# One table function for gelu, a fused bias and minimum in the scores, and probabilities scaled on ScalarE, in a two-layer encoder

## The chip, the cores and the metric

The kernel runs on one core of a Trainium2 chip. A core has five engines with queues of their own: TensorE (PE) for matmuls, VectorE (DVE) and ScalarE (ACT) for elementwise work, GpSimd (POOL), and SyncE (SP), which here issues DMAs. Each queue is worked off in order; semaphores tie the queues together. The metric is the device time of one execution in microseconds, the median over several runs.

## The reference

Two layers, each with two sub-layers, on one sequence of 256 tokens with 1024 channels in float32, then a last norm. Sub-layer 1 mixes tokens: one projection gives pooled groups, queries, keys and values of twelve heads in three dilation groups, and two gates. Sub-layer 2 is a gated MLP of width 2816 with a depthwise convolution of three tokens. What the change touches:

```python
# attention, for each head: logits with a bias, masked, a softmax
logits = jnp.einsum('bqhd,bqkhd->bhqk', qb, kb) * scale
logits = logits + bias[None, :, None, :]
logits = jnp.where(valid[None, None], logits, NEG_INF)
lse = jax.nn.logsumexp(logits, axis=-1)
p = jnp.exp(logits - lse[..., None])
o = jnp.einsum('bhqk,bqkhd->bqhd', p, vb)
...
wts = jax.nn.softmax(jnp.stack(lses, axis=0), axis=0)
...
merged = jax.nn.sigmoid(g_pool) * (pool_out @ w_a) + jax.nn.sigmoid(g_attn) * (attn_out @ w_b)
...
# the MLP: gelu is jax's default, the tanh form
a, gval = jnp.split(xn @ w_up, 2, axis=-1)
a = lax.conv_general_dilated(a, conv_w[:, None, :], ...) + conv_b
return (jax.nn.gelu(a) * gval) @ w_down
```

The three groups' outputs are combined by their softmax denominators, which is the same as one softmax over the concatenated logits of the three groups.

## The kernel before

Every matmul runs on float32 data in a faster format (float32r) and is split into a high and a low part, with three products (high by high, high by low, low by high). So each weight piece that comes from memory is split first: ScalarE casts the high part (`wh`, line 201), VectorE subtracts to get the low part (`wl`, line 203). The class `Weights` keeps that stream: loads from memory (three buffers `raw`, issued by SyncE), splits of pieces in the order of their use, up to three pieces ahead of the matmul that asks for one (`LOOK`), in at most five buffers (`BUFS`). A piece is 128 rows by 1024 columns' worth; `proj` (line 543) and `by_tokens`/`v_sum` (line 667) use it up, in 16 and 12 matmuls. The MLP's way down goes through `residual_mm` and `row_mm` (lines 585 to 587).

The program is written in the order in which the work is meant to happen, tile by tile; the framework orders the instructions of each engine, derives the semaphores, and `tc.issue_after` adds wishes by hand ("not before this one").

Attention in each layer: the projections of the six pairs of heads (`PAIRS`) run while a dictionary `steps` spreads the work of the four head slots (each with one head of each of the three groups) over twenty places. `scores(hh)` makes, for each of the two halves of tokens, a 128 by 512 tile of logits in PSUM (lines 1029 and 1034), adds the bias (`bias_of`, a strided view of a table; line 1040), takes the negated maximum of each row (line 1045), then the exponential with its sum (line 1048), the reciprocal of the sum (line 1050), and scales the probabilities by it and by one half (line 1051). That half comes from the gates: a sigmoid is made as half of (1 + tanh). `start_turn` transposes the probabilities in blocks on VectorE and sends them through memory with DMAs (`cross`, lines 711 to 718); `turn` splits the dense group's part into high and low (`pth` line 1072, `ptl` line 1073); `weigh` multiplies them with the values (lines 1082 and 1086) and splits the sum (`at2`, lines 1091 and 1092), which `by_tokens` uses later. Line 1131 and its neighbours evacuate the projections of queries and keys. `gate` (line 1160) makes the tanh of the gates.

The MLP works on 22 chunks of 128 channels. `up(f)` gets the chunk's activation from PSUM (`add_up`, lines 579 and 580; the first four come by another path, line 1266), makes the convolution (lines 1274, 1275 and 1278), then gelu out of a square (line 1288), a step on VectorE (1289), a tanh (1292) and another step (1293), multiplies by the gate's value and by one half (line 1297, or 1303 for the last two chunks) and splits the product (lines 1308 and 1309). The way down follows six chunks behind (`LAG`).

Line 756 is the first use of ScalarE at the start, line 771 the sum of squares of the input, line 918 the values' scaling by the first norm, line 372 a row of matmuls ahead of the real ones, lines 445 to 524 the residual sums and the last norm.

Of the kernel before, what the change touches and what calls it, by code (L numbers as in the profile page):

```python
# [10 lines left out]
F32 = mybir.dt.float32  # L11
F32R = mybir.dt.float32r
AF = mybir.ActivationFunctionType
ALU = mybir.AluOpType
AX = mybir.AxisListType

P = 128
# [224 lines left out]
def encoder(ctx, tc, x, w_in, w_pool, pool_scale, w_a, w_b, w_o, norm1, norm2, w_up, conv_w,  # L242
            conv_b, w_down, rel_bias, norm_f, onehot, edges, out):
    nc = tc.nc
# [3 lines left out]
    sm = ctx.enter_context(tc.tile_pool(name="small", bufs=2))  # L248
# [24 lines left out]
    for l in range(DEPTH):  # L273
        for g in range(NG):
            c0 = C_V + g * 512
            slots = (("m2", 0, 2), ("m2", 1, 2), ("ybig",), ("at2",)) if g == 0 else ()
            for j in range(2):
                tag = "k1" if l == 0 and g == 1 and j == 0 else None
# [25 lines left out]
        for j in range(2):  # L304
            tag = None if j else "k1"
# [4 lines left out]
        for f in range(4, NF, 2):  # L310
            if f in HALF_GROUPS:
                n, j = HALF_GROUPS[f]
                W.use(rows(w_up[l], j * 512, 4, DFF + n * 512, 512))
            a = cols(w_up[l], f * P)
            if f >= 4 * NQ:
                g = cols(w_up[l], DFF + f * P)
                a = [a[0], g[0], a[1], g[1]]
# [107 lines left out]
    def bias_of(t, hh):  # L425

        b = bt[:, hh]
        (pstep, pn), _ = b.ap
        blocks, first = (-2 * P, 4 * P - 1) if t == 0 else (-3 * P, 5 * P - 1)
        return bass.AP(b.tensor, b.offset + first, [[pstep, pn], [blocks, 2], [-1, 256]])  # L430
# [142 lines left out]
    def in_order(a):  # L573

        return a.rearrange("p (m t) -> p t m", t=2)
# [327 lines left out]
    for l in range(DEPTH):  # L903
# [25 lines left out]
        else:  # L929
            for g in range(NG):  # L930
                held = begun[0] if g == 0 else [W.get() for _ in range(4)]
                for t in range(2):
                    if g + t == 0:
                        ps = begun[1]
                    else:
                        ps = v_tile()
# [6 lines left out]
        if l == 0:  # L943
            load_params()
            with tc.issue_after(W.behind[1].ins):
                bias = build_bias()
# [6 lines left out]
        for gi in range(3, -1, -1):  # L953
# [12 lines left out]
            while sh < w:  # L966
# [3 lines left out]
                    out=nxt[:, :, 0:n], in0=cur[:, :, 0:n], in1=cur[:, :, sh : sh + n]  # L970
# [7 lines left out]
            if hw > 1:  # L978
# [5 lines left out]
                out=pd, in0=cur[:, :, o : o + S], scalar=1.0 / w, in1=u[:, :, PAD : PAD + S],  # L984
                op0=ALU.mult, op1=ALU.subtract,
# [39 lines left out]
        def scores(hh):  # L1025
            for t in range(2):
                ps = acc.tile([P, 512], F32, tag="acc", name="s_ps")
                for m, (a, b) in enumerate(((qh, kh), (qh, kl), (ql, kh))):
                    nc.tensor.matmul(  # L1029
                        ps[:, 0:256], a[:, hh, t, :], b[:, hh].rearrange("p t m -> p (t m)"),  # L1030
                        start=(m == 0), stop=(m == 2),
                    )
                for g in (1, 2):
                    nc.tensor.matmul(  # L1034
                        ps[:, 128 + g * 128 : 256 + g * 128], q[:, (g - 1) * HPG + hh, t, :],
                        kk[:, (g - 1) * HPG + hh, t, :],
                        start=True, stop=True,
                    )
                s = sm.tile([P, 512], F32, tag="s", name="s")
                nc.vector.tensor_add(  # L1040
                    out=s.rearrange("p (a b) -> p a b", a=2), in0=ps.rearrange("p (a b) -> p a b", a=2),
                    in1=bias_of(t, hh),
                )
                nm = sm.tile([P, 1], F32, tag="nm", name="nm")
                nc.vector.tensor_reduce(out=nm, in_=s, axis=AX.X, op=ALU.max, negate=True)
                z = sm.tile([P, 1], F32, tag="z", name="z")
                p = sm.tile([P, 512], F32, tag="p", bufs=3, name="p")
                nc.scalar.activation(p, s, AF.Exp, bias=nm[:, 0:1], accum_out=z)
                rz = sm.tile([P, 1], F32, tag="rz", name="rz")
                nc.vector.reciprocal(rz, z)  # L1050
                nc.vector.tensor_scalar(
                    out=p, in0=p, scalar1=rz[:, 0:1], scalar2=0.5, op0=ALU.mult, op1=ALU.mult
                )
                probs[hh, t] = p


# [19 lines left out]
        def weigh(hh):  # L1076
            pth, ptl, pt = ptiles[hh]
            ps = acc.tile([P, 2, P], F32, tag="acc", name="o_ps")
            for kc in range(2):
                c = slice(hh * P, (hh + 1) * P)  # L1080
                for m, (a, b) in enumerate(((vh, pth), (vh, ptl), (vl, pth))):
                    nc.tensor.matmul(ps, a[:, kc, c], b[:, kc], start=(kc + m == 0), stop=False)  # L1082
            for g in (1, 2):
                hd = (g - 1) * HPG + hh
                for t in range(2):
                    nc.tensor.matmul(  # L1086
                        ps[:, t, :], v[:, t, hd * P : (hd + 1) * P], pt[:, 4 * t : 4 * t + 4, 1 + g, :],
                        start=False, stop=(g == 2 and t == 1),
                    )
            oh, ol = at2[:, hh, 0], at2[:, hh, 1]  # L1090
            nc.scalar.copy(out=oh, in_=ps)
            nc.vector.tensor_sub(out=ol, in0=ps, in1=oh.bitcast(F32))


        steps = {
# [19 lines left out]
        for m, c in enumerate(PAIRS):  # L1115
# [7 lines left out]
            for n in range(4):  # L1123
# [4 lines left out]
                scale = HD**-0.5 if n < 2 else 1.0  # L1128
                if hd < HPG:
# [3 lines left out]
                        out=lo[:, hd], in0=src, scalar=scale, in1=hi[:, hd].bitcast(F32),  # L1133
                        op0=ALU.mult, op1=ALU.subtract,
                    )
                    nc.vector.scalar_tensor_tensor(
                        out=lo[:, hd], in0=rest, scalar=scale, in1=lo[:, hd].bitcast(F32),
                        op0=ALU.mult, op1=ALU.add,
                    )
                else:  # L1140
# [3 lines left out]
                        out=o, in0=src, scalar=scale, in1=o, op0=ALU.mult, op1=ALU.add  # L1144
# [6 lines left out]
        for cc in HALVES:  # L1151
            ps = by_tokens(po2, 4, then=step)
# [10 lines left out]
        for cc in HALVES:  # L1163
# [4 lines left out]
            for t in range(2):  # L1168
                nc.vector.scalar_tensor_tensor(
                    out=pa[:, t, cc], in0=th[:, t], scalar=1.0, in1=pa[:, t, cc],  # L1170
                    op0=ALU.add, op1=ALU.mult,
# [5 lines left out]
        for n, cc in enumerate(HALVES):  # L1177
            th = gate()
            ps = by_tokens(at2, 2, 2)
            ks = slice(4 * n, 4 * n + 4)  # L1180
            y = big.tile([P, 2, 4, 4, 32], F32, tag=("q0", "k0")[n], name="turned")
            z = big.tile([P, 2, 4, 4, 32], F32, tag=("q1", "v0")[n], name="merged")
# [53 lines left out]
        z_of = [zg[:, 0], zg[:, 1], zga[:, 0]]  # L1236
# [6 lines left out]
        def of_chunk(z, i):  # L1243
            return z[:, :, i].rearrange("p (t a) j -> p t a j", t=2)
# [17 lines left out]
        def up(f):  # L1262
            w0, w1, w2, b = (prm[:, l, j * NF + f : j * NF + f + 1] for j in range(4))
            a = sm.tile([P, S], F32, tag="u", name="a")
            if f < 4:
                nc.scalar.copy(
                    out=a.rearrange("p (a j t) -> p t a j", t=2, j=32), in_=of_chunk(za, f)
                )
            else:
                sums = proj(x2, 2)  # L1270
                with W.after_splits():
                    add_up(in_order(a), [halves(b) for b in sums])
            y = sm.tile([P, S], F32, tag="s", name="y")
            nc.scalar.activation(y, a, AF.Identity, bias=b, scale=w1)
            nc.vector.scalar_tensor_tensor(
                out=y[:, 1:], in0=a[:, : S - 1], scalar=w0, in1=y[:, 1:], op0=ALU.mult, op1=ALU.add
            )
            nc.vector.scalar_tensor_tensor(
                out=y[:, : S - 1], in0=a[:, 1:], scalar=w2, in1=y[:, : S - 1],
                op0=ALU.mult, op1=ALU.add,  # L1280
            )
            g = sm.tile([P, 2, P], F32, tag="p", bufs=3, name="g")
            if f >= 4 * NQ:
                add_up(g, [halves(a) for a in proj(x2, 2)])

            c = float(np.sqrt(2.0 / np.pi))
            y2 = sm.tile([P, S], F32, tag="us", name="y2")
            nc.scalar.activation(y2, y, AF.Square, scale=float(np.sqrt(0.044715)))
            nc.vector.scalar_tensor_tensor(
                out=y2, in0=y2, scalar=1.0, in1=y, op0=ALU.add, op1=ALU.mult  # L1290
            )
            nc.scalar.activation(y2, y2, AF.Tanh, scale=c)
            nc.vector.scalar_tensor_tensor(
                out=y2, in0=y2, scalar=1.0, in1=y, op0=ALU.add, op1=ALU.mult
            )
            if f < 4 * NQ:
                nc.vector.scalar_tensor_tensor(  # L1297
                    out=g.rearrange("p t (a j) -> p t a j", j=32),
                    in0=y2.rearrange("p (a j t) -> p t a j", t=2, j=32), scalar=0.5,
                    in1=of_chunk(z_of[f // 4 % 3], f % 4), op0=ALU.mult, op1=ALU.mult,  # L1300
                )
            else:
                nc.vector.scalar_tensor_tensor(
                    out=g, in0=in_order(y2), scalar=0.5, in1=g, op0=ALU.mult, op1=ALU.mult
                )
            n = f % NH
            ah, al = (x[n >= HPG][:, n - HPG * (n >= HPG)] for x in (acth, actl))
            nc.scalar.copy(out=ah, in_=g)  # L1308
            nc.vector.tensor_sub(out=al, in0=g, in1=ah.bitcast(F32))
            acts[f] = (ah, al)  # L1310
# [64 lines left out]
```

## Time and profile before

| What | Value |
|---|---|
| time before, median of 3 runs | 859.94 us |
| the three runs | 859.94, 860.45, 859.87 us |
| span of the profiled execution, first to last instruction | 858.0 us |
| granted TensorE clock, mean over the span | 0.998 |
| DMA | 186.81 MB, 218 GB/s on average |
| one instruction of the table loads of ScalarE (ACT_TABLE_LOAD) | 1 in the whole run |

The profile is a record of one execution. The page gives the busy time of each engine, the chain of work that ended last, and groups of instructions by line. "PE" is TensorE's matmuls, "PEld" its weight loads, which overlap them. In a row of a group, `x44 | 17.8, 420 | 1.6 <-ACT y L1292 0.8` says: 44 instructions, 17.8 us busy, 420 ns each on average; before them the engine sat idle for 1.6 us, 0.8 us of it until ScalarE's line 1292 was done. A row of the chain in order of time gives the start in us, the length in us, and what ran. A row of the timeline gives start, length, engine, line, operation, tiles and shapes, how many are merged, and in brackets the idle time before. A row of the waits names who waited for whom: total us, times, longest.

### The profile page before, as it was taken

The numbers are of one execution on the slowest core, as the hardware profiler recorded it, in microseconds if no ns is written. First come the engines' busy times: TensorE is split into PE (matmuls) and PEld (weight loads), VectorE is DVE, ScalarE is ACT, GpSimd is POOL, SyncE is SP. The second block draws the span as 40 slices with busy tenths as digits, with TensorE's granted clock in tenths as the row PEclk, the third lists the DMA queues.
The fourth block names the chain that finished last, engine by engine and source line by source line (L and its number), as shares of the span: only waits on it lengthen the run. The fifth ranks groups of instructions, "written<-read, shape, count | busy, mean of one in ns | idle before, by whom it ended". The sixth has DMA issues, their size and how long they took to land.

```text
span 858.0 us, 11823 instructions
## 1 busy us (share of the span) xinstructions
PE 851.6 (99%) x4343; PEld 727.9 (85%) x4343; DVE 661.2 (77%) x1050; ACT 493.8 (58%) x795; POOL 32.0 (4%) x98
## 2 busy tenths in 40 slices
PE   9999999999999999999999999999999999999997
PEld 8888888888888888888888889988888888888886
DVE  7998796667767788888855987874776777988894
ACT  7756654455445476666645665543654555775672
POOL 1710000000010000000000000000000000000001
PEclk9999999999999999999999999999999999999999
DMA  9686547766747876666736555658667478676641
GB/s 331 217 248 206 196 163 231 240 228 229 250 182 246 270 249 231 231 235 206 245 99 209 184 199 192 198 175 268 226 243 275 154 249 259 246 256 208 239 147 49
DMA packets 136387, 186.81 MB, mean 218 GB/s; under 512 B 5561, under 2 KB 88193, under 8 KB 136329
## 3 DMA queue, kind: packets, MB, share of 16 engines
q1 hardware_dynamic: 136168, 185.79, 63.8%
q8 instruction: 34, 0.56, 0.3%
q10 hardware_dynamic: 160, 0.27, 0.1%
q14 instruction: 25, 0.20, 0.1%
HBM read 172.39 MB, written 13.65 MB: 217 GB/s over the span
## 4 chain that ended last, share of the span: by engine, by line
PE 99%; DVE 0%; ACT 0%; POOL 0%; issue 0%; POOLq 0%; ACTq 0%
PE proj_ps L543 34%; PE t_ps L667 30%; PE v_ps L667 6%; PE res_ps L586 6%; PE res_ps L585 6%; PE res_ps L587 6%; PE v_ps L895 3%; PE v_ps L802 1%; PE pool_ps L543 1%; PE o_ps L1086 1%; PE s_ps L1034 1%; PE s_ps L1029 1%; PE o_ps L1082 1%; PE xt_ps L481 1%; PE gain_ps L372 0%; PE xt_ps L750 0%
## 5 line engine op out<-in xcount | busy, mean ns | idle before, releaser
L203 DVE TENSOR_TENSOR wl<-raw,wh 128x1024 fp32r<-128x1024 f32 x274 | 329.8, 1217 | 88.1 <-ACT wh L201 73.6
L201 ACT CAST wh<-raw 128x1024 fp32r<-128x1024 f32 x274 | 284.3, 1049 | 118.3 <-PE t_ps L667 49.0
L543 PE MATMUL proj_ps<-x,wh 128*128 128x512 f32 x832 | 196.9, 390 | 0.0
L543 PEld LDWEIGHTS proj_ps<-x,wh 128*128 128x128 f32 x832 | 154.3, 188 | 30.9
L667 PE MATMUL t_ps<-wh,x 128*128 128x512 f32 x576 | 179.7, 390 | 0.0
L667 PEld LDWEIGHTS t_ps<-wh,x 128*128 128x128 f32 x576 | 107.8, 188 | 22.3
L667 PE MATMUL t_ps<-wl,x 128*128 128x512 f32 x288 | 112.1, 389 | 0.0
L543 PEld LDWEIGHTS proj_ps<-x,wl 128*128 128x128 f32 x832 | 105.4, 191 | 3.0
L543 PE MATMUL proj_ps<-x,wl 128*128 128x256 f32 x832 | 107.8, 283 | 0.0
L586 PE MATMUL res_ps<-wl,actq 128*128 128x512 f32 (+1 forms) x184 | 70.0, 380 | 0.0
L587 PE MATMUL res_ps<-wh,actk 128*128 128x512 f32 (+1 forms) x184 | 69.9, 380 | 0.0
L585 PE MATMUL res_ps<-wh,actq 128*128 128x512 f32 (+1 forms) x184 | 69.7, 381 | 0.0
L667 PEld LDWEIGHTS t_ps<-wl,x 128*128 128x128 f32 x288 | 54.1, 188 | 11.2
L667 PE MATMUL t_ps<-wh,po 128*128 128x512 f32 x128 | 41.4, 395 | 0.0
L587 PEld LDWEIGHTS res_ps<-wh,actk 128*128 128x128 f32 x184 | 34.6, 188 | 6.6
L586 PEld LDWEIGHTS res_ps<-wl,actq 128*128 128x128 f32 x184 | 34.6, 188 | 6.4
L585 PEld LDWEIGHTS res_ps<-wh,actq 128*128 128x128 f32 x184 | 34.5, 188 | 6.3
L454 POOL TENSOR_SCALAR ss<-ss 128x1 f32<-128x1 f32 x8 | 2.0, 253 | 779.6 <-ACT junk L447 779.6
L1308 ACT CAST actq<-g 128x256 fp32r<-128x256 f32 x44 | 17.0, 403 | 20.7 <-DVE g L1297 20.0
L667 PEld LDWEIGHTS t_ps<-wh,po 128*128 128x128 f32 x128 | 24.0, 188 | 4.9
L447 ACT ACTIVATE junk<-h 128x512 f32<-128x512 f32 (+1 forms) x19 | 10.5, 553 | 28.6 <-DVE h L445 28.5
L579 ACT COPY a<-proj_ps 128x256 f32<-128x256 f32 x36 | 13.6, 389 | 23.3 <-PE proj_ps L543 23.3
(204 smaller groups left out, 1148.9 us busy)
## 6 DMA issues: line engine op xcount, KB each, us to landing
raw<-in_w_in_dram SPq DMA_DIRECT2D x58, 1024.0 KB, 5.4
raw<-in_w_up_dram SPq DMA_DIRECT2D x44, 1024.0 KB, 6.9
raw<-in_w_down_dram SPq DMA_DIRECT2D x22, 1024.0 KB, 4.7
raw<-in_w_a_dram SPq DMA_DIRECT2D x8, 1024.0 KB
raw<-in_w_o_dram SPq DMA_DIRECT2D x8, 1024.0 KB, 7.1
crossing<-crossing SPq DMA_DIRECT2D x12, 512.0 KB, 5.4
turning<-turning SPq DMA_DIRECT2D x8, 512.0 KB, 2.8
turned_p<-turning SPq DMA_DIRECT2D x32, 128.0 KB, 3.3
```

What stands on the lines that cost most here:

```text
L201: inst = nc.scalar.copy(out=h, in_=src)
L203: inst = nc.vector.tensor_sub(out=l, in0=src, in1=h.bitcast(F32))
L447: nc.scalar.activation(junk[:, 0 : cc.stop - cc.start], h[:, t, cc], AF.Square, scale=D**-0.5, accum_out=ss[:, n : n + 1],)
L481: nc.tensor.transpose(pt[:, k, :], xn[:, c0 : c0 + P], ident)
L543: nc.tensor.matmul(out, w(k), x, start=(steps is first and k == 0), stop=(steps is last and k == nk - 1), skip_group_check=turns["rest"],)
L579: nc.scalar.copy(out=out, in_=sums[1])
L585: nc.tensor.matmul(ps, ah, wh, start=first, stop=False, skip_group_check=on)
L586: nc.tensor.matmul(ps, ah, wl, start=False, stop=False, skip_group_check=on)
L587: nc.tensor.matmul(ps, al, wh, start=False, stop=last, skip_group_check=on)
L667: nc.tensor.matmul(ps, x2[:, 2 * n + j, part, t, :], w[:, j, :], start=(n + m == 0), stop=(n == last and m == 5),)
L895: nc.tensor.matmul(ps[t], a[:, k, t, :], w[:, j, :], start=(k + m == 0), stop=(k == KD - 1 and m == 2),)
L1308: nc.scalar.copy(out=ah, in_=g)
```

## The change

In `scores`, the addition of the bias and the maximum become one VectorE instruction that writes the negated sums and the minimum of each row of them, which is the negated maximum; the exponential then takes them with a scale of −1. The probabilities are scaled by the reciprocal on ScalarE instead of VectorE, without the one half. In `weigh`, the half is applied to the weighed sum. In the MLP's `up`, gelu's four steps become one ScalarE table function (the tanh form), and the product with the gate loses its half.

```diff
@@ scores
                 s = sm.tile([P, 512], F32, tag="s", name="s")
-                nc.vector.tensor_add(
+                nm = sm.tile([P, 1], F32, tag="nm", name="nm")
+                nc.vector.tensor_tensor_reduce(
                     out=s.rearrange("p (a b) -> p a b", a=2), in0=ps.rearrange("p (a b) -> p a b", a=2),
-                    in1=bias_of(t, hh),
-                )
-                nm = sm.tile([P, 1], F32, tag="nm", name="nm")
-                nc.vector.tensor_reduce(out=nm, in_=s, axis=AX.X, op=ALU.max, negate=True)
+                    in1=bias_of(t, hh), scale=-1.0, scalar=3.0e38, op0=ALU.add, op1=ALU.min, accum_out=nm,
+                )
                 z = sm.tile([P, 1], F32, tag="z", name="z")
                 p = sm.tile([P, 512], F32, tag="p", bufs=3, name="p")
-                nc.scalar.activation(p, s, AF.Exp, bias=nm[:, 0:1], accum_out=z)
+                nc.scalar.activation(p, s, AF.Exp, bias=nm[:, 0:1], scale=-1.0, accum_out=z)
                 rz = sm.tile([P, 1], F32, tag="rz", name="rz")
                 nc.vector.reciprocal(rz, z)
-                nc.vector.tensor_scalar(
-                    out=p, in0=p, scalar1=rz[:, 0:1], scalar2=0.5, op0=ALU.mult, op1=ALU.mult
-                )
+                nc.scalar.mul(out=p, in_=p, mul=rz[:, 0:1])
                 probs[hh, t] = p
@@ weigh
             oh, ol = at2[:, hh, 0], at2[:, hh, 1]
-            nc.scalar.copy(out=oh, in_=ps)
-            nc.vector.tensor_sub(out=ol, in0=ps, in1=oh.bitcast(F32))
+            nc.scalar.mul(out=oh, in_=ps, mul=0.5)
+            nc.vector.scalar_tensor_tensor(
+                out=ol, in0=ps, scalar=0.5, in1=oh.bitcast(F32), op0=ALU.mult, op1=ALU.subtract
+            )
@@ up
-            c = float(np.sqrt(2.0 / np.pi))
             y2 = sm.tile([P, S], F32, tag="us", name="y2")
-            nc.scalar.activation(y2, y, AF.Square, scale=float(np.sqrt(0.044715)))
-            nc.vector.scalar_tensor_tensor(
-                out=y2, in0=y2, scalar=1.0, in1=y, op0=ALU.add, op1=ALU.mult
-            )
-            nc.scalar.activation(y2, y2, AF.Tanh, scale=c)
-            nc.vector.scalar_tensor_tensor(
-                out=y2, in0=y2, scalar=1.0, in1=y, op0=ALU.add, op1=ALU.mult
-            )
+            nc.scalar.activation(y2, y, AF.Gelu_apprx_tanh)
             if f < 4 * NQ:
-                nc.vector.scalar_tensor_tensor(
+                nc.vector.tensor_mul(
                     out=g.rearrange("p t (a j) -> p t a j", j=32),
-                    in0=y2.rearrange("p (a j t) -> p t a j", t=2, j=32), scalar=0.5,
-                    in1=of_chunk(z_of[f // 4 % 3], f % 4), op0=ALU.mult, op1=ALU.mult,
+                    in0=y2.rearrange("p (a j t) -> p t a j", t=2, j=32),
+                    in1=of_chunk(z_of[f // 4 % 3], f % 4),
                 )
             else:
-                nc.vector.scalar_tensor_tensor(
-                    out=g, in0=in_order(y2), scalar=0.5, in1=g, op0=ALU.mult, op1=ALU.mult
-                )
+                nc.vector.tensor_mul(out=g, in0=in_order(y2), in1=g)
```

## The prediction

> **What bounds the kernel now.** I read the page's share of busy time and its chain first, then the waits with TensorE alone, then the chain in order of time, to see whether a busy TensorE hides stalls.
>
> ```profile
> span 858.0 us, 11823 instructions
> PE 851.6 (99%) x4343; PEld 727.9 (85%) x4343; DVE 661.2 (77%) x1050; ACT 493.8 (58%) x795; POOL 32.0 (4%) x98
> ```
>
> ```profile
> PE 99%; DVE 0%; ACT 0%; POOL 0%; issue 0%; POOLq 0%; ACTq 0%
> ```
>
> ```profile
> PE gain_ps L372 <- PEq L1357: 0.8, 1, 0.8
> ```
>
> ```profile
> 40.62 33.38 PE proj_ps L543 x192
> 463.74 33.34 PE proj_ps L543 x192
> 846.76 0.70 DVE h L445
> ```
>
> The chain that ends last is 99% TensorE, and TensorE's only wait in 858 us is the 0.8 us before its first instruction. Matmul ends are modelled, so "busy" alone proves little; the rhythm proves more. The same 192 matmuls of line 543 take 33.38 us in layer 0 and 33.34 us in layer 1, though different work of VectorE and ScalarE lies beside them. So TensorE runs at its own pace from 0.8 to 846.76 us, and behind it lies a tail of 858.0 − 846.8 = 11.2 us (last norm and stores), which the change doesn't touch. All three edits concern VectorE and ScalarE. They can pay nothing directly; they can only cost, by making TensorE wait. The question is what cover each edited instruction has.
>
> **The change, part by part.** Durations (mean ns of one) of what is removed and of the nearest relatives of what is added:
>
> ```profile
> L1293 DVE SCALAR_TENSOR_TENSOR y<-y,y 128x256 f32<-128x256 f32 x44 | 17.8, 420 | 1.6 <-ACT y L1292 0.8
> L1309 DVE TENSOR_TENSOR actk<-g,actq 128x256 fp32r<-128x256 f32 x44 | 17.8, 420 | 4.3 <-ACT actq L1308 3.2
> L1292 ACT ACTIVATE y<-y 128x256 f32<-128x256 f32 x44 | 17.5, 414 | 4.7 <-DVE y L1289 4.3
> L1040 DVE TENSOR_TENSOR s<-s_ps,bt 128x512 f32<-128x512 f32 x16 | 10.8, 684 | 4.2 <-PE s_ps L1034 4.1
> L1045 DVE TENSOR_REDUCE nm<-s 128x1 f32<-128x512 f32 x16 | 10.5, 677 | 0.1
> L1051 DVE TENSOR_SCALAR p<-p,rz 128x512 f32<-128x512 f32 x16 | 7.4, 483 | 0.1
> L918 ACT ACTIVATE v<-v_ps,rstd 128x512 f32<-128x512 f32 x4 | 2.7, 687 | 3.3 <-PE v_ps L895 3.3
> L1048 ACT ACTIVATE p<-s,nm 128x512 f32<-128x512 f32 x16 | 11.5, 720 | 13.8 <-DVE nm L1045 13.8
> L1091 ACT CAST at<-o_ps 128x256 fp32r<-128x256 f32 x8 | 2.9, 365 | 15.7 <-PE o_ps L1086 15.7
> L1131 ACT ACTIVATE qh<-proj_ps 128x256 fp32r<-128x256 f32 x8 | 3.1, 383 | 2.3 <-PE proj_ps L543 2.3
> L756 ACT ACT_TABLE_LOAD x1 | 1.3, 1283 | 1.3 <-PEq L1357 1.3
> ```
>
> ```profile
> L771 DVE SCALAR_TENSOR_TENSOR junk<-h x2: 684/684/685, 10.1 to 10.7; 128x512 f32<-128x512 f32 x2
> L771 DVE DVE_READ_ACCUMULATOR junk<-h x2: 82/82/82, 10.7 to 11.3; 128x1 f32 x2
> ```
>
> *Gelu.* Each of 44 chunks loses one of two ScalarE functions of 256 elements (line 1292: 414 ns) and two VectorE steps of three operands (line 1293: 420 ns). The product with the gate, a step of that same kind and size, turns into a plain product of two, which line 1309 prices as another plain step at 420 too: nothing. VectorE −44 × 2 × 0.420 = −37.0 us, ScalarE −44 × 0.414 = −18.2 us. The gelu itself lies between nothing saved by the new function (414, as any function there) and line 1048's 720, which has twice the elements and a pointer; I take 414, since form and size are line 1292's.
>
> *Bias and minimum.* The trace has no instruction that combines and reduces in one pass over PSUM. Nearest is line 771, a product with a sum beside it: 684 ns and 82 for reading the accumulator. The bounds are 684 (line 1040 alone) and 684 + 677 = 1361 (a fused form at half pace, no gain). I take 766 by line 771. VectorE −16 × (684 + 677 − 766) = −9.5 us; at the other end 0.
>
> The Trainium skill, page "Vector Engine (DVE) Microarchitecture Reference", section 7, warns that the accumulating form with two non-bf16 sources in SBUF runs at half throughput. Line 771 is of that kind and took 684 ns, as long as a plain sum of 512 elements, so the trace doesn't agree; by the rule VectorE's sum below would be −44.7 us instead of −54.2.
>
> *Scaling.* VectorE −16 × 483 = −7.7 us; ScalarE gains a multiplication by a pointer on 512 elements, between 687 (line 918) and 720 (line 1048): 16 × 0.70 = +11.2 us. Halving moves to lines 1091 and 1092: 365 becomes 383 (line 1131, a multiplication from PSUM), 0.02 us later, and the three-operand subtraction costs what the plain one does.
>
> *Table loads.* Square, Exp, Tanh and the copies live today with one load of 1283 ns in the whole run. Should gelu belong to another table, there are three more: before the first gelu of each layer and before layer 1's first Exp, ScalarE +3.8 us.
>
> Sums: VectorE −37.0 − 9.5 − 7.7 = −54.2 us, ScalarE −18.2 + 11.2 + 3.8 = −3.2 us. On TensorE's path: 0.
>
> *What the new waits hold up.* The scaling now crosses from VectorE (reciprocal) to ScalarE and back to the transposes; behind the waiting ScalarE stand the evacuation of the next projection (line 1131) and the weight casts (line 201), for which VectorE's low parts (line 203) wait, and then TensorE.
>
> ```profile
> 111.39 1.21 DVE L203 TENSOR_TENSOR wl<-raw,wh 128x1024 fp32r<-128x1024 f32 x1
> 112.52 0.21 DVE L1050 RECIPROCAL rz<-z 128x1 f32<-128x1 f32 x2
> ...
> 116.03 2.34 DVE L203 TENSOR_TENSOR wl<-raw,wh 128x1024 fp32r<-128x1024 f32 x2
> ```
>
> ```profile
> 121.71 11.11 PE proj_ps L543 x64
> ```
>
> A low part stands ahead of the reciprocals on VectorE, so ScalarE may stall some 1.2 us at a pair of score tiles, and their scaling takes 2 × 0.70 where VectorE took 2 × 0.48. Against that, the low part finished at 117.2 (first of the pair of 116.03) is first read when the projection of 121.71 runs: 4.5 us of cover. The stall ends on no matmul: 0; without that cover it would be 1.2 us for each of eight pairs, 9.6 us.
>
> The loads: ScalarE sat idle ahead of these places anyway.
>
> ```profile
> 271.94 0.42 ACT L1288 ACTIVATE y<-y 128x256 f32<-128x256 f32 x1 [1.16 <-DVE y L1278]
> 533.99 0.73 ACT L1048 ACTIVATE p<-s,nm 128x512 f32<-128x512 f32 x1 [3.10 <-DVE nm L1045]
> ```
>
> ```profile
> 274.25 1.23 DVE L203 TENSOR_TENSOR wl<-raw,wh 128x1024 fp32r<-128x1024 f32 x1 [0.51 <-ACT wh L201]
> 300.37 1.22 DVE L203 TENSOR_TENSOR wl<-raw,wh 128x1024 fp32r<-128x1024 f32 x1 [1.68 <-ACT wh L201]
> ```
>
> ```profile
> 259.23 38.08 PE t_ps L667 x168
> ...
> 303.31 0.23 PE res_ps L586
> ```
>
> The first row is layer 0's first function of gelu, the second layer 1's first Exp; layer 1's MLP repeats layer 0's. Of 1.283 us at most 0.12 is exposed on ScalarE, and the low part of 274.25, done at 275.48, belongs to the ninth weight piece of the run of line 667 that starts at 259.23; at twelve matmuls a piece, each 38.08 / 168 = 0.227, that is read from 259.23 + 96 × 0.227 = 281.0: 5.5 us of cover. The MLP's thinnest cover is 303.31 − 301.59 = 1.7 us (the low part of 300.37 before line 586 reads it), and there VectorE loses work. Without cover the loads would cost 3 × 1.283 = 3.8 us.
>
> The place with the least cover is the end of attention:
>
> ```profile
> 175.59 0.12 PE o_ps L1082
> 175.71 0.70 PE t_ps L667 x3
> 176.41 0.59 PE o_ps L1082 x5
> ```
>
> ```profile
> 177.93 0.37 ACT L1091 CAST at<-o_ps 128x256 fp32r<-128x256 f32 x1 [6.82 <-PE o_ps L1086]
> 178.20 2.00 ACT L201 CAST wh<-raw 128x1024 fp32r<-128x1024 f32 x2
> 179.28 2.36 DVE L203 TENSOR_TENSOR wl<-raw,wh 128x1024 fp32r<-128x1024 f32 x2 [0.52 <-ACT wh L201]
> 180.95 0.39 PE L667 MATMUL t_ps<-wl,x 128*128 128x512 f32 x1
> ```
>
> Two weight casts stand in ScalarE's queue behind line 1091, which sat 6.82 us until the last head's output was summed. The first low part is done at 179.28 + 1.22 = 180.50, and TensorE reads it at 180.95: 0.45 us. Line 1091's 0.02 us more leaves 0.43.
>
> **Sum.** The profiled run spans 858.0 us; the runs' median is 859.94, so 1.9 us lie around the span. Change on the path 0: 858.0 stays, and I write 860.0.
>
> **Rivals.**
>
> *A. The queues are filled in another order (slower).* The code writes the six matmuls of line 1082 in one row, but the trace shows three matmuls of another line inside the six. So the order on each engine comes from a planner that reckons with durations and readiness, and the new instructions have new ones. If the last head's output falls behind one more weight piece, twelve matmuls, line 1091 and the casts behind it start 12 × 0.227 = 2.72 us later, against 0.43 of cover: 2.3 us in each layer, 864.5 in all. It decides from a shift of two matmuls. For it: the cover, and that these matmuls were placed where the last head's low part was expected. Against: the new score path is shorter on VectorE, which pulls that output forward as easily.
>
> *B. The table loads fall on TensorE.* Three loads in places without cover: 859.9 + 3.8 = 863.8. Against it, the idle stretches and 5.5 us above.
>
> [...]
>
> *C. Loads back and forth.* If the copies, squares and Identity weren't in gelu's table, each chunk would load twice, 88 × 1.283 = 113 us of ScalarE. Two chunks then add 5.1 us, against covers of 1.7 to 5.5 us: an estimated 0.4 us of stall for each of 44 chunks, some 877. Against it: today's single load already serves every kind the kernel has, so the cheap ones aren't tied to one function.
>
> *D. Faster.* TensorE would have to gain 1.7 us though it doesn't wait. Only a pace loosened by less traffic beside it could do that; the two layers' 33.38 and 33.34 us say 0.04 in 33, a whole run's worth 1 us: 859.
>
> *E. The fused instruction saves nothing* (1361 ns). VectorE stays 9.5 us busier, off the path: 860.0, the forecast's time.
>
> **How the numbers follow.** Forecast with E: 0.61. A 0.27, B 0.05, C 0.04, D over 0.2%: 0.03. What can be told from no change is 0.2%, 1.7 us. Slower by more: A + B + C, without such small shifts as stall under 0.85 us a layer, which stay inside 0.2% and are in the 0.61: 0.36. Faster 0.03. The range reaches down to D's 859.0 and up past A's 864.5 to 864.8; outside are C and the larger shifts of A, some 0.15. The forecast's own range is 859.0 to 861.6.
>
> **What would show it.** Right: the chain stays 99% TensorE, TensorE's waits show nothing beyond the start, VectorE's busy time falls to about 607 us and ScalarE's to about 491, ACT_TABLE_LOAD counts four, the fused instruction takes about 684 ns plus 82. Wrong by A: gaps before line 667 matmuls near 180 and 604 us, with weight splits as releasers. By B: gaps within 3 us behind a load. By C: some ninety loads. Wrong altogether: a span that moves while TensorE shows no wait, which would mean that its pace isn't its own.

## The result and the profile after

| | before | changed |
|---|---|---|
| median of 13 runs, us | 860.02 | 862.39 |
| span of the profiled execution, us | 858.0 | 860.5 |

The changed kernel takes 1.003 times the time of the kernel before (95% interval 1.0022 to 1.0039): 2.4 us slower. That is more than the 0.2% that the prediction counted as no change, and less than rival A's 864.5.

The head of the page and the waits of TensorE, changed kernel:

```profile
span 860.5 us, 11694 instructions
...
PE 852.6 (99%) x4343; PEld 728.3 (85%) x4343; DVE 618.8 (72%) x946; ACT 492.8 (57%) x770; POOL 32.7 (4%) x98
...
PE 95%; DVE 2%; ACT 1%; issue 1%; DMA 1%; POOL 0%; POOLq 0%; ACTq 0%
```

```profile
PE v_ps L667 <- DVE x L485: 0.8, 2, 0.4
PE gain_ps L372 <- PEq L1346: 0.8, 1, 0.8
PE xt_ps L481 <- DVE xn L472: 0.5, 1, 0.5
```

And those of its weight loads at the same places:

```profile
PEld v_ps L667 <- DVE x L485: 1.7, 2, 0.8
PEld xt_ps L481 <- DVE xn L472: 0.7, 1, 0.7
```

VectorE is 42 us less busy, and TensorE's busy share still reads 99%. But the chain is no longer TensorE alone, and TensorE now waits in three places, always for VectorE: twice for line 485, once for line 472. Both lines belong to the norms that the change doesn't touch. Line 485 makes the low part of the normalised activations `x` that the next matmuls read; line 472 scales the rows that TensorE transposes.

TensorE's own waits look too small for 2.4 us: the weight loads of the same matmuls wait too, the two overlap, and matmul ends are modelled, so neither can be read as the loss. The rhythm tells the size. Four runs of matmuls that both kernels have alike serve as milestones. In the chain in order of time (start, length, what), changed kernel first, then the one row of the kernel before that was not shown yet:

```profile
40.91 33.38 PE proj_ps L543 x192
...
260.09 38.08 PE t_ps L667 x168
...
465.60 33.34 PE proj_ps L543 x192
...
684.74 38.08 PE t_ps L667 x168
```

```profile
682.29 38.08 PE t_ps L667 x168
```

Each run takes exactly as long as before; only the starts move.

| From milestone to milestone, us | before | changed | difference |
|---|---|---|---|
| start to 1 | 40.62 | 40.91 | +0.29 |
| 1 to 2 (attention, layer 0's second norm) | 218.61 | 219.18 | +0.57 |
| 2 to 3 (MLP, step to layer 1) | 204.51 | 205.51 | +1.00 |
| 3 to 4 (attention, layer 1's second norm) | 218.55 | 219.14 | +0.59 |
| 4 to the end | 175.71 | 175.76 | +0.05 |

They add up to 2.5 us, the difference of the spans. The first 0.29 isn't the change: in the traces TensorE, VectorE, ScalarE and GpSimd run the same instructions in the same order up to the first scores (108 us) in both kernels, and the profiled runs of all ten kernels put milestone 1 anywhere from 40.51 to 42.55.

**Layer 0's second norm.** VectorE's timeline (start, length, engine, line), kernel before and then changed kernel:

```profile
245.84 0.41 DVE L631 TENSOR_TENSOR h<-res_ps,h 128x256 f32<-128x256 f32 x1
246.17 0.68 DVE L485 TENSOR_TENSOR x<-xt_ps,x 128x512 fp32r<-128x512 f32 x1
246.77 1.21 DVE L203 TENSOR_TENSOR wl<-raw,wh 128x1024 fp32r<-128x1024 f32 x1
```

```profile
246.22 0.42 DVE L631 TENSOR_TENSOR h<-res_ps,h 128x256 f32<-128x256 f32 x1
246.55 1.22 DVE L203 TENSOR_TENSOR wl<-raw,wh 128x1024 fp32r<-128x1024 f32 x1
247.69 0.69 DVE L485 TENSOR_TENSOR x<-xt_ps,x 128x512 fp32r<-128x512 f32 x1
```

And TensorE's, kernel before and then changed kernel:

```profile
246.94 1.64 PE L667 MATMUL v_ps<-v,x 128*128 128x512 f32 x6
```

```profile
247.33 0.71 PE L667 MATMUL v_ps<-v,x 128*128 128x512 f32 x2
248.43 1.20 PE L667 MATMUL v_ps<-v,x 128*128 128x512 f32 x4 [0.39 <-DVE x L485]
```

The same three instructions, in another order: the weight split of 1.22 us, whose result TensorE first reads at about 252 us, stands ahead of the 0.69 us that TensorE needs at once. Two matmuls run on the high part, the third reads the low part. In the kernel before, the low part was done at 246.85 and the third matmul, the third of the six in the row, started at 247.49; in the changed kernel it stalls until the low part is done at 248.38. Nothing here got longer by more than 0.01 us.

**The step to layer 1.** The same view, kernel before and then changed kernel:

```profile
423.70 0.69 DVE L445 TENSOR_TENSOR h<-res_ps,h 128x512 f32<-128x512 f32 x1 [1.35 <-PE res_ps L587]
424.30 1.22 DVE L203 TENSOR_TENSOR wl<-raw,wh 128x1024 fp32r<-128x1024 f32 x1
426.25 1.28 DVE L472 SCALAR_TENSOR_TENSOR xn<-h,rstd,gain 128x256 f32<-128x256 f32 x3 [0.73 <-POOL rstd L459]
```

```profile
424.47 1.23 DVE L203 TENSOR_TENSOR wl<-raw,wh 128x1024 fp32r<-128x1024 f32 x1 [1.94 <-ACT wh L201]
425.62 0.69 DVE L445 TENSOR_TENSOR h<-res_ps,h 128x512 f32<-128x512 f32 x1
428.14 0.48 DVE L472 SCALAR_TENSOR_TENSOR xn<-h,rstd,gain 128x256 f32<-128x256 f32 x1 [1.84 <-POOL rstd L459]
428.54 0.69 DVE L445 TENSOR_TENSOR h<-res_ps,h 128x512 f32<-128x512 f32 x1
429.14 1.27 DVE L472 SCALAR_TENSOR_TENSOR xn<-h,rstd,gain 128x256 f32<-128x256 f32 x3
```

TensorE's transposes of the scaled rows, kernel before and then changed kernel:

```profile
427.65 0.60 PE L481 MATMUL xt_ps<-ident,xn 128*128 128x128 f32 x4
```

```profile
428.77 0.41 PE L481 MATMUL xt_ps<-ident,xn 128*128 128x128 f32 x2
429.68 0.44 PE L481 MATMUL xt_ps<-ident,xn 128*128 128x128 f32 x2 [0.49 <-DVE xn L472]
```

Here the split is at the head of an in-order queue and itself waits 1.94 us for ScalarE's cast, while the residual sum behind it (line 445) could have run about 1.7 us earlier (423.70 in the kernel before, where all of this lies 0.2 us earlier). The sum of squares, the root and the scaled rows follow from that sum, and the first row is 1.9 us late. A second change of order goes with it: the next residual sum (428.54) now stands between the first scaled row and the second, for which the third transpose waits, so that one starts only at 429.14. What cover there was leaves 1.00 us on TensorE.

**What was added.** Groups by line, and line 1041 by itself (min, median and max in ns), changed kernel:

```profile
L1286 ACT ACTIVATE y<-y 128x256 f32<-128x256 f32 x44 | 17.3, 413 | 9.5 <-DVE y L1277 9.4
L1050 ACT ACTIVATE p<-p,rz 128x512 f32<-128x512 f32 x16 | 10.9, 717 | 2.1 <-DVE rz L1049 2.1
L1286 ACT ACT_TABLE_LOAD x2 | 2.6, 1283 | 3.5 <-DVE y L1277 3.5
L756 ACT ACT_TABLE_LOAD x1 | 1.3, 1283 | 1.3 <-PEq L1346 1.3
L1047 ACT ACT_TABLE_LOAD x1 | 1.3, 1283 | 0.0
```

```profile
L1041 DVE DVE_READ_ACCUMULATOR2_ANT nm<- x16: 81/83/88, 109.9 to 579.6; 128x1 f32 x16
L1041 DVE CUSTOM_DVE_ANT_0 s<-s_ps,bt x8: 681/686/692, 109.3 to 577.2; 128x512 f32<-128x512 f32 x8
```

Gelu costs 413 ns, the fused instruction 686 (the other eight of the sixteen carry a second name and take 685) and 83 for its accumulator, the scaling 717, and there are four table loads of 1283 ns.

### The profile page after: what moved, and what is told of

Its sections match the earlier page's. It is cut to its first block, busy times and chain, and to the rows that moved or that the text cites. A ratio compares the mean times of both kernels' runs of the same rounds, so it can differ in the third digit from the quotient of the medians.

```text
span 860.5 us, 11694 instructions
## 1 busy us (share of the span) xinstructions
PE 852.6 (99%) x4343; PEld 728.3 (85%) x4343; DVE 618.8 (72%) x946; ACT 492.8 (57%) x770; POOL 32.7 (4%) x98
## 4 chain that ended last, share of the span: by engine, by line
PE 95%; DVE 2%; ACT 1%; issue 1%; DMA 1%; POOL 0%; POOLq 0%; ACTq 0%
PE proj_ps L543 33%; PE t_ps L667 30%; PE v_ps L667 6%; PE res_ps L587 5%; PE res_ps L585 5%; PE res_ps L586 5%; PE v_ps L895 3%; PE v_ps L802 1%; PE pool_ps L543 1%; PE o_ps L1083 1%; PE s_ps L1034 1%; PE s_ps L1029 1%; PE o_ps L1079 1%; DVE h L445 1%; DMA raw<-in_w_in_dram 1%
## 5 line engine op out<-in xcount | busy, mean ns | idle before, releaser
L580 DVE TENSOR_TENSOR a<-proj_ps,a 128x256 f32<-128x256 f32 x36 | 15.0, 423 | 24.5 <-ACT a L579 24.4
```

Of the source, the lines that this page charges most:

```text
L580: nc.vector.tensor_add(out=out, in0=sums[0], in1=out)
```

## The experiments

All are compared with the kernel before on the same chip. The queue orders quoted in the expectations were read from the built programs before the runs; they show, instruction by instruction, what each edit does to VectorE's queue at the three places, and the traces show the same orders. The ratio in each result is the measured one of the runs, with its 95% interval; it need not be the exact quotient of the two medians.

### The gelu edit alone

```diff
-            nc.scalar.activation(y2, y, AF.Square, scale=float(np.sqrt(0.044715)))
...
+            nc.scalar.activation(y2, y, AF.Gelu_apprx_tanh)
```

> Kernel before with the gelu edit alone. Theory Q (the loss comes from where the planner puts one weight split among the norm's VectorE steps): in its VectorE queue only the step from layer 0 to layer 1 has the changed kernel's order (the split ahead of the second residual sum), so TensorE loses 0.9 to 1.0 us there and nothing at layer 0's second norm; layer 1's second norm has a third order, 0 to 0.3 us. Time 860.9 to 861.3. Rival L (ScalarE's three further table loads cost their time): three loads are here as well, so all of the 2.4 us, 862.4. Rival S (the score edits cost): 860.0.

Measured: 861.14 us against 859.94 (ratio 1.0011, 1.0003 to 1.002). TensorE's waits in its trace:

```profile
PE gain_ps L372 <- PEq L1347: 0.8, 1, 0.8
PE xt_ps L481 <- DVE xn L472: 0.5, 1, 0.5
```

One wait behind the start, at the step to layer 1: between the milestones −0.02, +1.01 and −0.18 us. At layer 1's second norm 0 to 0.3 us of loss were expected, and the stretch is 0.18 shorter. All three further table loads are in this kernel and it bears only that one place's loss.

### Both score edits, old gelu

```diff
+                nc.vector.tensor_tensor_reduce(
...
+                nc.scalar.mul(out=p, in_=p, mul=rz[:, 0:1])
...
+            nc.scalar.mul(out=oh, in_=ps, mul=0.5)
```

> Kernel before with both score edits (fused bias and minimum, probabilities scaled on ScalarE, half moved) and the old gelu. Theory Q: both second norms have the changed kernel's order (the split ahead of the first low part of x), 0.65 us each, the step between the layers has the order of before: 861.2 to 861.4. Rival L: one table load, 860.0. Rival S: 862.4.

Measured: 861.13 us against 859.94 (1.0014, 1.0005 to 1.0023), a little under the expected 861.2. Its waits are the complement:

```profile
PE v_ps L667 <- DVE x L485: 0.8, 2, 0.4
PE gain_ps L372 <- PEq L1356: 0.8, 1, 0.8
```

Between the milestones +0.57, −0.03 and +0.59. So the whole loss splits cleanly: gelu owns the step between the layers, the scores own the two second norms. Neither place holds an instruction of the edit that owns it.

### The whole change, with the order mended

```diff
+                    if t == 0 and psum is acc:
+                        W.queue_behind((last[1],), 1, first_up[l][0] + 3)
                     yield
...
-                nc.vector.tensor_add(out=h[:, t, cc], in0=ps, in1=h[:, t, cc])
+                added = nc.vector.tensor_add(out=h[:, t, cc], in0=ps, in1=h[:, t, cc])
+                if self.ahead is None and l == 0 and t == 0 and n == 1 and W.n_split > first_up[0][0] + 8:
+                    W.queue_behind((added,), 1, values[1] + 4)
```

`values[1]` is the number of the first piece of layer 1's values.

> The changed kernel, with two wishes for VectorE's queue: the fourth piece of the MLP's first weights is split behind the first low part of x at each second norm, and the fifth piece of layer 1's first weights behind layer 0's second residual sum. No work is added or left out. Theory Q: the time of before, 859.9 to 860.4, with no wait of TensorE near 247, 428 and 671 us. Rivals L and S: 862.4, the order of three instructions being a symptom.

Measured: 859.89 us against 859.94 (0.9997, 0.9988 to 1.0006), at the lower edge of what was expected. Its waits, and VectorE at layer 0's second norm (line 488 is the low part of `x` here):

```profile
PE gain_ps L373 <- PEq L1351: 0.8, 1, 0.8
PE v_ps L807 <- DVE m L219: 0.2, 1, 0.2
```

```profile
246.16 0.68 DVE L488 TENSOR_TENSOR x<-xt_ps,x 128x512 fp32r<-128x512 f32 x1
246.76 1.22 DVE L203 TENSOR_TENSOR wl<-raw,wh 128x1024 fp32r<-128x1024 f32 x1
```

Both waits lie at the start (line 807 is a matmul of the first values). The three differences are −0.10, −0.01 and −0.09 us. Two ordering wishes that add no work take back the whole loss, with all the change's instructions, four table loads included, still there. Against the changed kernel's trace every engine but VectorE runs the same instructions in the same order from start to end, and VectorE's order differs at these three places alone.

### The kernel before, with the order spoilt

```diff
+                first = psum is acc and t == n == 0
+                high = nc.scalar.copy(out=oh, in_=pt)
+                if first:
+                    yield
+                    W._split(first_up[l][0] + 4)
+                with tc.issue_after(W.last[1].ins) if first else ExitStack():
+                    last = [high, nc.vector.tensor_sub(out=ol, in0=pt, in1=oh.bitcast(F32))]
```

> The kernel before, with none of the change, but at each second norm the first low part of x is put behind the split of that fourth piece. Theory Q: 0.5 to 0.65 us lost at 247 and at 670, 861.0 to 861.3. Rivals L and S: 860.0.

Measured: 861.01 us against 859.94 (1.0013, 1.0004 to 1.0022), and +0.51, −0.01, +0.50 us between the milestones.

```profile
PE v_ps L670 <- DVE x L489: 0.8, 2, 0.4
```

The wait of the changed kernel, for the same instruction at both norms, without any of the change. Against the trace of the kernel before, the place of one split at each second norm is the only difference in the order of any engine. This shows the cause from the other side, at two of the three places; the third was not spoilt in the kernel before.

### One wish at a time

The changed kernel with the first of the two wishes:

> The changed kernel with the wish at the two second norms alone. Theory Q: the 2 x 0.63 us there are gone, the 0.9 us between the layers stay: 860.8 to 861.2, TensorE's wait at 428 us (for the norm's scaled rows) is left as the only one behind the start.

Measured: 860.97 us against 860.05 (1.0012, 1.0004 to 1.0021); −0.10, +1.04, −0.07 us. With the second:

> The changed kernel with the wish between the layers alone. Theory Q: the 2 x 0.63 us at the second norms stay, the rest is gone: 861.0 to 861.4, TensorE waits near 247 and 671 us for the low part of x, not near 428.

Measured: 861.11 us against 860.05 (1.0015, 1.0006 to 1.0024); +0.58, −0.04, +0.60 us. Its profiled run reached milestone 1 only at 42.55 us, 1.9 later than the kernel before, so its span (861.1) says less here than the differences and the runs do.

### Each score edit alone

The fused instruction alone, and the scaling on ScalarE (with the half behind the weighed sum) alone:

> Kernel before with the fused bias and minimum alone. In its queue the split stands behind the first low part of x, as in the kernel before, with one residual sum between them. Theory Q: nothing lost, 859.8 to 860.3. Rival A1 (each score edit costs its share of the 1.2 us by itself, as work): about 860.5.

> Kernel before with the probabilities scaled on ScalarE and the half moved behind the weighed sum, alone. The same order at the norms as with the fused instruction alone. Theory Q: nothing lost, 859.8 to 860.3, though ScalarE has 16 more instructions of 0.7 us. Rival A1: about 860.5.

Measured: 859.74 and 859.68 us against 860.05 (both 0.9997, 0.9988 to 1.0006), a little under the expected 859.8; each shows −0.20, about 0 and −0.18 us between the milestones. So the 1.2 us of the two together is not the sum of two prices: alone, neither moves the split ahead of the low part of `x`; together they do.

No version beat the kernel before by more than the measurement can tell.

## Why the prediction was right or wrong

**Right: what bounds the kernel.** TensorE's runs of matmuls kept their lengths to 0.00 us, and 42 us less of VectorE's work bought nothing, as "They can pay nothing directly" said.

**Right, nearly: the prices.** The fused instruction was predicted at 766 ns and took 686 + 83 = 769; the scaling 700 against 717; gelu 414 against 413; the halving 383 against 379; four table loads. VectorE's busy time fell by 42.4 us instead of 54.2 (neighbours overlap in the timeline, 245.84 + 0.41 ends after 246.17, and a sum of durations counts such stretches twice: added up over all groups, count times mean, VectorE's durations fall by 51.7, from 722.4 to 670.7, so the overlaps make up most of the gap), ScalarE's by 1.0 instead of 3.2 (added up, 2.6). The rule of the Trainium skill's "Vector Engine (DVE) Microarchitecture Reference" (section 7) can't be judged by the fused instruction: the rule speaks of two sources in SBUF, and this one, at 686 ns, has one in PSUM. So the prediction's −44.7 put the rule where it doesn't apply.

**Wrong: the forecast of no change.** The step that failed is "Change on the path 0", and the search for the place "with the least cover" behind it. I measured cover for weight splits alone: how long before its matmul a low part is done. The norms' own steps, which stand on the same VectorE queue, were put at nothing without being measured. In the kernel before, line 485 ended at 246.85 and the third matmul of the run from 246.94 started at 247.49: 0.64 us of cover. That is more than the 0.43 at the end of attention, but a split put ahead moves line 485 by 1.14 us (246.55 to 247.69), and the 0.5 us that are not covered are what the kernel with the order spoilt lost at each norm. Measured were 0.57, 1.00 and 0.59 us at the three places in place of 0. The 862.39 lies inside the stated range of 859.0 to 864.8 by luck: that range was stretched to rival A's time, for a loss at another place, and the forecast's own ended at 861.6.

**Half right: rival A.** Its mechanism, another filling of the queues, is what the runs show; that it comes from the durations of the new instructions was argued, not shown. Its place and price were wrong. At the end of attention the order did change, but to the better. The chain of the changed kernel:

```profile
168.57 5.49 PE t_ps L667 x24
174.06 0.71 PE o_ps L1079 x6
```

The last head's output comes after 24 matmuls instead of 32 with 3 more inside it, so the casts behind it start 2.2 us earlier (ScalarE's line 1088 at 175.70, against 177.93). The loss came where A didn't look, at 0.6, 1.0 and 0.6 us instead of 2.3 a layer.

**Right, for the wrong reason: the table loads (rival B).** I let the load run in ScalarE's idle time and counted at most 0.12 us of it as exposed. ScalarE's timeline of the changed kernel:

```profile
272.79 1.28 ACT L1286 ACT_TABLE_LOAD   x1 [1.84 <-DVE y L1277]
274.08 0.42 ACT L1286 ACTIVATE y<-y 128x256 f32<-128x256 f32 x1
...
532.36 0.38 ACT L1130 ACTIVATE qh<-proj_ps 128x256 fp32r<-128x256 f32 x1 [0.58 <-PE proj_ps L543]
532.76 1.28 ACT L1047 ACT_TABLE_LOAD   x1
534.67 0.72 ACT L1047 ACTIVATE p<-s,nm 128x512 f32<-128x512 f32 x1 [0.62 <-DVE nm L1041]
```

At gelu the load started only when VectorE's step was done, so all of its 1.28 us came behind the wait; at the exponential it ran ahead of the wait, as I had assumed. The weight cast behind the first gelu began at 274.40 against 273.18 in the kernel before; with the 0.86 us by which the run of matmuls at this place starts later, that leaves 0.4 us, since fewer functions stand ahead of the cast now. The cover of 5.5 us took it: the kernel with both wishes has all four loads and loses nothing. At gelu the function starts as the load ends (272.79 + 1.28 = 274.07). At the exponential the load starts 0.02 us after the function ahead of it ended (532.36 + 0.38 = 532.74), and the 0.62 us behind it are a wait for VectorE. So the drain of about 1.38 us that the Trainium skill's "ScalarE: Activation LUTs" ("What ACT_TABLE_LOAD costs") adds to a load shows behind neither load, nor ahead of the second; at gelu the wait ahead could hide one.

**C and E.** No loads back and forth: two rows of line 1286 for 44 gelus. The fused instruction does save what it should.

**D.** TensorE did not gain. The orders that the three edits give one by one are 0.2 us shorter at some norms than the kernel before; that is far inside what the runs can tell.

What stays open is by what reckoning the planner turns the three places: that the order follows from the edits is seen in the built programs and in the traces, but not what tips each choice.

## What to carry to other kernels

When one engine is busy for 99% of the span and never waits, as here, taking work off the others has nothing to win but can cost, because the planner that orders the queues may reorder stages that were not touched. Measure cover for everything that the busy engine waits on, the small norm steps too, and compare the orders of the queues before and after. Where a long instruction that is not urgent shares a queue with a short urgent one, fix their order in the program by an explicit wish.

## What was not expected of the hardware

A table load stood behind the wait of the function it serves in one place (272.79, after 1.84 us of idling) and ahead of it in another (532.76, then 0.62 us of idling), so whether an idle stretch hides it must be read from the trace.

The start scatters: with queues that are the same up to the first scores, the same matmuls began between 40.51 and 42.55 us in ten profiled runs, 2.0 us, nearly as much as the whole effect studied here. Differences between milestones told it where spans alone would have misled.
